# Memory's value projections moved from the front of the kernel to the dense blocks behind the mixer, with the front reordered and the convolution's taps dealt out anew

## The chip, the cores and the metric

The kernel runs on one core of a Trainium2 chip. The metric is the device time of one execution in microseconds, the median of several executions. The engines are TensorE (PE), VectorE (DVE), ScalarE (ACT), GpSimd (POOL) and SyncE (SP, which only issues transfers here). A 0.3% difference is about 3.9 us.

## What is computed

Two transformer blocks in a row on x (512 tokens by 1024), all in fp32. Of the reference only what the change touches is shown:

```python
# first block: adaptive norm, the front of the kernel
mod = c @ w_ada + b_ada                       # shift, scale, gate
h = rmsnorm(x, norm_g) * (1 + scale) + shift
proj = h @ w_in                               # q_a, k_a, v_a, z_a, ...

# second block: mixer's convolution branch and its end
c = u[..., :512] * sigmoid(u[..., 512:])
c = silu(layernorm(causal_dwconv(c, cv_dw_w) + cv_dw_b))   # 31 taps, 512 channels
y = concat([a, c]);  h = h + y @ w_out
# second block: cross attention to 256 memory rows
m = rmsnorm(mem, norm_mem_g)
kv = m @ w_ckv                                # 1024 columns of keys, 1024 of values
```

The memory's keys and values depend on the inputs `mem` and `w_ckv` alone, so they can be computed at any time before the cross attention.

## The kernel before, in words

**Products.** Each fp32 product is made of three matmuls on a high and a low part (high by high, high by low, low by high). Weights come in units of 512 KB: SP issues the load into `wr` (three buffers), ACT casts the high part `wh` (L162), DVE or POOL subtracts to get the low part `wl` (L163; a string of D and P says which engine takes which unit), then PE runs the unit's matmuls (L144). The load for a unit's buffer is issued when the unit three before it has been split.

**Front (L467 to L527).** An order written out by hand for all five engines. SP loads the vectors, the memory `mr`, x transposed (`xt`), 16 weight units for the memory and 16 rows `ar` for `mod`. A loop over n = 0 to 16 takes in each step one unit of memory weights: eight for keys (24 matmuls of 128x256 each), then eight for values (24 of 128x256 each, two units to a PSUM bank); results are copied out by ACT (`kvo`) and written to DRAM (`kv_d`) by DMAs that POOL issues. Between them stand, by tables of step numbers, the 16 rows of `mod` on DVE (`ada`, L440, one multiply and sum over 128x1024 each, ACT then forms shift or gain), the sums of squares of x (ACT squares, DVE adds to `xacc`) and of memory, the two inverse roots with their broadcasts (`bch`, `bcl`), and eight token chunks: `y` (DVE L462, one buffer in PSUM), high part (ACT L464), low part (DVE L466). The q and k projections of the first attention follow; the first of their transposes or the value projection (`z<-wh,h`) begins when they are done.

**Dense blocks (L1185 to L1221).** A list `BLOCKS` of weight units gives PE's order; `AFTER` names the attention steps that follow a unit. The convolution's 31 taps of each of four channel chunks are dealt to PE (units `cd`, 8 taps and 24 matmuls of 128x512 each), DVE (L1051, accumulating in PSUM) and POOL (L1046, with a product by ACT before it). A sum `ca` of both parts follows (L1057), then the layer norm over channels: the mean by PE (L1069), squares by ACT with 16 column sums on PE (`ones,cpr`), an inverse root, a broadcast and SiLU. Units `wo2a` multiply the attention half by `w_out`, units `wo2c` (L1232) the convolution half, and the cross attention's projections come next. DVE and POOL taps wait in two queues (`fill_v`, `fill_p`) from which some are issued after each unit.

## Time and profile before

| | |
|---|---|
| median of 3 runs | 1296.67 us (1294.57 to 1297.94) |
| the profiled execution | 1296.6 us, span 1294.8 us |
| mean granted TensorE clock | 0.971 of full speed |
| busy share of PE, DVE, ACT, POOL | 95%, 58%, 46%, 36% |
| DMA | 136.44 MB, mean 105 GB/s |

The profiled execution stands at the median, so a sum made against its trace can be read against the median as it is. PE is nearly always busy; it is below nine tenths in the first slices of the page (the front) and in those around 650 to 780 us (the end of the mixer), and the granted clock is below full in the same places. A matmul's busy time includes what overlaps with the next one; so the starts of matmuls, not their durations, tell how fast PE goes.

### The profile page before, as it was taken

What the parts mean: (1) busy time and instruction counts of PE and PEld (TensorE: products, weight loads), DVE (VectorE), ACT (ScalarE), POOL (GpSimd) and SP (SyncE); (2) the same over time, 40 slices, a digit from 0 to 9 for tenths busy, and PEclk for the clock granted to TensorE, in tenths of its full rate; (3) what the DMA queues carried; (4) which work ended last, traced back from release to release, by engine and by line L of the source; (5) the groups of instructions that cost most, each with busy time, mean ns of one, the idle gap of its engine ahead of it and who ended that gap; (6) DMA issues with size and microseconds to landing.
All of it is one profiled execution on the core that took longest, in us unless ns stands there. A gap on an engine that the chain in (4) does not pass through costs nothing.

```text
span 1294.8 us, 16902 instructions
## 1 busy us (share of the span) xinstructions
PE 1233.2 (95%) x6412; PEld 1039.3 (80%) x6412; DVE 750.5 (58%) x1216; ACT 601.6 (46%) x994; POOL 466.3 (36%) x315
## 2 busy tenths in 40 slices
PE   8799999999999999999899678999999999999996
PEld 6789887988887888899777566887888888888886
DVE  6654777666465174355877338456587777771112
ACT  7444557555652345264645436444444444442221
POOL 0573453332222138332537727104422222222222
PEclk8899999999999999999999779999999999999998
DMA  9853232232258432222122204312233333322221
GB/s 348 322 167 103 80 90 74 66 90 82 66 155 266 121 127 98 73 84 73 57 58 74 73 33 130 97 34 67 96 98 98 98 98 98 98 90 90 94 85 66
DMA packets 43859, 136.44 MB, mean 105 GB/s; under 512 B 4993, under 2 KB 8577, under 8 KB 43778
## 3 DMA queue, kind: packets, MB, share of 16 engines
q1 hardware_dynamic: 43010, 133.26, 32.3%
q0 software_dynamic: 768, 2.10, 0.4%
q8 instruction: 51, 0.84, 0.3%
q14 instruction: 30, 0.25, 0.1%
HBM read 125.90 MB, written 6.29 MB: 102 GB/s over the span
## 4 chain that ended last, share of the span: by engine, by line
PE 78%; DVE 9%; ACT 5%; POOL 4%; issue 3%; DMA 2%; SPq 0%; DVEq 0%; ACTq 0%; POOLq 0%
PE lin L144 64%; PE z L144 7%; PE pv L144 3%; PE sm L144 2%; DMA wr<-in_wts 1%; PE z L604 1%; POOL wl L163 1%; ACT wh L162 1%; DVE sm L1051 1%; DVE wl L163 1%; POOL rb L1046 1%; POOL nacc L1046 1%; DVE h L221 1%; DVE om L689 0%; DMA mr<-in_mem_t 0%
## 5 line engine op out<-in xcount | busy, mean ns | idle before, releaser
L144 PE MATMUL lin<-h,wh 128*128 128x512 f32 (+1 forms) x2264 | 699.0, 389 | 15.9 <-ACT wh L162 10.5
L144 PEld LDWEIGHTS lin<-h,wh 128*128 128x128 f32 x2264 | 420.4, 190 | 102.2 <-ACT wh L162 13.6
L163 POOL TENSOR_TENSOR wl<-wr,wh 128x1024 fp32r<-128x1024 f32 (+1 forms) x116 | 281.0, 2423 | 453.1 <-ACT wh L162 425.6
L144 PE MATMUL lin<-h,wl 128*128 128x512 f32 (+1 forms) x1132 | 437.6, 387 | 5.3 <-POOL wl L163 3.9
L162 ACT CAST wh<-wr 128x1024 fp32r<-128x1024 f32 (+1 forms) x198 | 205.5, 1041 | 266.2 <-PE lin L144 178.6
L144 PEld LDWEIGHTS lin<-h,wl 128*128 128x128 f32 x1132 | 215.1, 190 | 48.6 <-POOL wl L163 5.0
L163 DVE TENSOR_TENSOR wl<-wr,wh 128x1024 fp32r<-128x1024 f32 (+1 forms) x82 | 108.9, 1328 | 125.2 <-ACT wh L162 124.3
L144 PE MATMUL lin<-wh,h 128*128 128x256 f32 x672 | 130.3, 291 | 2.3 <-DVE h L985 2.3
L144 PEld LDWEIGHTS lin<-wh,h 128*128 128x128 f32 x672 | 109.5, 197 | 2.5 <-issue 2.4
L1346 DVE SCALAR_TENSOR_TENSOR cv<-up,vecs,cv 128x512 f32<-128x512 f32 x88 | 94.6, 1075 | 17.9 <-ACT cv L1344 16.4
L144 PE MATMUL lin<-wl,h 128*128 128x256 f32 x336 | 97.4, 290 | 1.8 <-POOL wl L163 1.8
L144 PE MATMUL lin<-zz,wh 128*128 128x512 f32 (+1 forms) x324 | 91.9, 369 | 0.0
L144 PEld LDWEIGHTS lin<-wl,h 128*128 128x128 f32 x336 | 66.3, 197 | 2.1 <-POOL wl L163 2.0
L144 PEld LDWEIGHTS lin<-zz,wh 128*128 128x128 f32 x324 | 58.1, 187 | 11.6
L144 PE MATMUL lin<-zz,wl 128*128 128x512 f32 (+1 forms) x162 | 59.7, 369 | 0.0
L317 POOL TENSOR_TENSOR nacc<-nacc,sq 128x512 f32<-128x512 f32 x34 | 53.4, 1578 | 15.9 <-ACT sq L316 15.4
L1341 POOL MEMSET up<- 128x2 f32 x44 | 4.3, 100 | 148.7 <-DVE cv L1346 116.6
L675 POOL TENSOR_TENSOR zs<-zs,y 64x512 f32<-64x512 f32 x16 | 26.4, 1653 | 72.4 <-DVE y L674 70.0
L1353 ACT ACTIVATE cv<-cv 128x512 f32<-128x512 f32 x22 | 13.9, 632 | 60.0 <-DVE cv L1346 60.0
L689 DVE TENSOR_TENSOR_SCAN om<-om 128x511 f32<-128x511 f32 (+3 forms) x32 | 36.7, 1187 | 8.4 <-ACT om L685 8.1
L1342 DVE TENSOR_TENSOR up<-lin,rb 128x512 f32<-128x512 f32 x44 | 30.1, 686 | 16.3 <-PE lin L144 13.7
L214 DVE TENSOR_TENSOR tl<-z,th 128x512 fp32r<-128x512 f32 (+1 forms) x60 | 33.3, 595 | 10.8 <-ACT th L213 10.4
(392 smaller groups left out, 1701.2 us busy)
## 6 DMA issues: line engine op xcount, KB each, us to landing
wr<-in_wts SPq DMA_DIRECT2D x198, 512.0 KB, 3.5
ar<-in_wts SPq DMA_DIRECT2D x16, 512.0 KB, 6.3
qk<-qk SPq DMA_DIRECT2D x24, 128.0 KB, 2.3
wr<-in_wts SPq DMA_DIRECT2D x8, 384.0 KB, 3.0
xt<-in_x_t SPq DMA_DIRECT2D x4, 512.0 KB, 8.2
kv_d<-kvo POOLq DMA_DIRECT2D x16, 128.0 KB, 4.9
ma_d<-gt SPq DMA_DIRECT2D x8, 256.0 KB, 4.4
ma<-ma_d SPq DMA_DIRECT2D x8, 256.0 KB, 2.9
```

Of the source, the lines that this page charges most:

```text
L144: pe.matmul(o, lhsT=lhsT, rhs=rhs, start=start, stop=stop, skip_group_check=True)
L162: act.copy(out=hi[:, :n], in_=raw[:, :n])
L163: lo_engine().tensor_tensor(out=lo[:, :n], in0=raw[:, :n], in1=f32(hi[:, :n]), op=ALU.subtract)
L214: dve.tensor_tensor(out=lo, in0=src, in1=f32(hi), op=ALU.subtract)
L221: dve.scalar_tensor_tensor(out=lo, in0=src, scalar=g, in1=f32(hi), op0=ALU.mult, op1=ALU.subtract)
L317: pool.tensor_tensor(out=acc, in0=acc, in1=q, op=ALU.add)
L675: pool.tensor_tensor(out=zs[r], in0=zs[r], in1=y[r], op=ALU.mult)
L689: dve.tensor_tensor_scan(out=om[:, o:e], data0=om[:, o:e], data1=om[:, o:e], initial=1.0, op0=ALU.mult, op1=ALU.bypass)
L1046: pool.tensor_tensor(out=cb_, in0=cb_, in1=pr, op=ALU.add)
L1342: dve.tensor_tensor(out=up[:, :T], in0=o, in1=rb[:, 0], op=ALU.mult)
L1346: dve.scalar_tensor_tensor(out=r, in0=up[:, 2 - j:2 - j + T], scalar=V("ffn_w", c * 3 + j), in1=r, op0=ALU.mult, op1=ALU.add)
L1353: act.activation(out=a, in_=a, func=AF.Silu)
```

## The change

- The front computes only the eight key units (`N_FRONT` 8). Its low parts are made by DVE for the first two units and by POOL for six.
- x's sums of squares are formed by PE: ACT squares eight chunks into buffers, PE sums each over the channels by a column of ones. Memory's squares are summed the same way, 16 such matmuls in place of three DVE adds and two matmuls; DVE copies the result to `mrc`. The inverse root and the broadcast of `mrc` are written later in the program, but are not under the manual order, and stand in the front of DVE all the same.
- The rows of `mod` are loaded earlier and come two to a step; the token chunks start at step 4 instead of 9.
- The memory's split tiles (hi and lo, 2.1 MB) are written to DRAM (`ms_d`) by eight DMAs of SP and read back in the dense blocks by eight more (`memory_back`).
- Eight units `mv` (24 matmuls of 128x256 each) stand between the last blocks of `BLOCKS`.
- Unit `cd:4` is gone: each chunk has eight taps on PE. Of chunks 2 and 3 DVE gets 14 taps each (before 12 and 4), POOL 9 each (before 11).
- The low parts of the last blocks alternate between POOL and DVE (`B2_LO`); the steps of the layer norm come after `wo2a:0`, `wo2a:1` and `mv:6`, and only the first of them flushes the queues.

```diff
-CV_UNITS = (1, 1, 1, 2)
+CV_UNITS = (1, 1, 1, 1)
-START_LO = "DDDDDDDDPPPPPPPP"
+START_LO = "DDPPPPPP"
+N_FRONT = 8
-ADA_LOADS = (2, 1, 1, 2, 1, 1, 2, 1, 1, 2, 1, 1)
-NORM_AT = (6, 9)
-H_AT = (9, 10, 11, 12, 13, 14, 16, 16)
+SQ_AT = (0, 0, 1, 1, 1, 2, 2, 2)
+ADA_LOADS = (4, 2, 2, 2, 2, 2, 2)
+NORM_AT = (3, 5)
+H_AT = (4, 5, 5, 6, 6, 7, 8, 8)
-B2_LO = "P"
+B2_LO = 26 * "P" + 5 * "PD"
-CONV_POOL = (8, 8, 11, 11)
+CONV_POOL = (8, 8, 9, 9)
-          "u2:7 cd:2 cd:3 cd:4 wo2a:0 wo2a:1 wo2a:2 wo2a:3")
+          "u2:7 cd:2 mv:0 cd:3 mv:1 mv:2 mv:3 wo2a:0 mv:4 wo2a:1 mv:5 wo2a:2 mv:6 wo2a:3 mv:7")
-         21: "n3", 22: "o3", 27: "l0", 28: "l1"}
+         21: "n3", 22: "o3", 28: "l0", 30: "l1", 33: "l2"}
...
     def memory_norm():
         o = ps_sm()
-        for i in range(2):
-            mm(o[:, i:i + 1], raws[0][:, i * P:(i + 1) * P], ones[:, 0:1], True, True)
-        rsq(mrc, o[:, :2], D)
+        for k in range(KD):
+            for i in range(2):
+                mm(o[:, i:i + 1], raws[k // 4][:, (k % 4) * NM + i * P:(k % 4) * NM + (i + 1) * P], ones[:, 0:1],
+                   k == 0 and i == 0, k == 7)
+        dve.tensor_copy(out=mrc, in_=o[:, :2])
...
+    def sums_x(k, q):
+        for i in range(NT):
+            mm(xs_[:, i:i + 1], q[:, i * P:(i + 1) * P], ones[:, 0:1], k == 0 and i == 0, k == 7)
...
+    for i, t in enumerate(mt):
+        nc.sync.dma_start(out=ms_d[i], in_=f32(t))
...
+    def memory_back():
+        for i in range(4):
+            hi, lo = htile(), htile()
+            nc.sync.dma_start(out=f32(hi), in_=ms_d[2 * i])
+            nc.sync.dma_start(out=f32(lo), in_=ms_d[2 * i + 1])
...
-            fill(FILL_P if i < 22 else 5, fill_p)
-        norm_out()
+            fill(FILL_P if i < 22 else 4, fill_p)
```

In the changed kernel the line numbers differ: L440 becomes L412, L462 and L466 become L435 and L439, L1046 becomes L1060, L163 becomes L166.

SP's queue in the front, before, from the memory's load on (`mr` memory, `wr` weight units, `xt` chunks of x, `lamt` and `posi` small inputs, `ar` rows of `mod`):

```order
L349 DMA mr<-in_mem_t 128x4x256 x2
L149 DMA wr<-in_wts 128x1024 x2
L448 DMA xt_83<-in_x_t 128x2x512
L149 DMA wr<-in_wts 128x1024
L448 DMA xt_83<-in_x_t 128x2x512 x2
L712 DMA lamt<-in_lam 128x256
L725 DMA posi<-in_pos 128x4
L149 DMA wr<-in_wts 128x1024
L448 DMA xt_83<-in_x_t 128x2x512
L149 DMA wr<-in_wts 128x1024 x2
L435 DMA ar<-in_wts 128x1024 x2
L149 DMA wr<-in_wts 128x1024
```

The same stretch of SP's queue in the changed kernel:

```order
L353 DMA mr<-in_mem_t 128x4x256 x2
L152 DMA wr<-in_wts 128x1024 x2
L420 DMA xt_83<-in_x_t 128x2x512
L152 DMA wr<-in_wts 128x1024
L420 DMA xt_83<-in_x_t 128x2x512 x2
L505 DMA ms_d<-h 128x512 x8
L693 DMA lamt<-in_lam 128x256
L706 DMA posi<-in_pos 128x4
L152 DMA wr<-in_wts 128x1024
L420 DMA xt_83<-in_x_t 128x2x512
L152 DMA wr<-in_wts 128x1024 x2
L407 DMA ar<-in_wts 128x1024 x4
```

The eight writes of `ms_d` stand ahead of the fourth weight unit, and four rows `ar` come at once where two came before.

DVE's queue in the front, before, from the second pair of `mod` rows (`ar,mod`) behind x's inverse root to the row behind the first `y`; `rv`, `rq` and `mrc` are the memory's inverse root:

```order
L440 SCALAR_TENSOR_TENSOR ar,mod<-ar,cb 128x1024 x2
L294 TENSOR_TENSOR bcl<-xrc,bch 128x4
L440 SCALAR_TENSOR_TENSOR ar,mod<-ar,cb 128x1024 x2
L287 TENSOR_SCALAR rv<-sm 128x2
L262 RECIPROCAL mrc<-rq 128x2
L263 TENSOR_TENSOR rq<-mrc 128x2
L264 TENSOR_TENSOR rq<-rq,rv 128x2
L265 TENSOR_SCALAR rq<-rq 128x2
L266 TENSOR_TENSOR mrc<-mrc,rq 128x2
L440 SCALAR_TENSOR_TENSOR ar,mod<-ar,cb 128x1024
L462 SCALAR_TENSOR_TENSOR y<-xt_83,gain,xrb 128x512
L440 SCALAR_TENSOR_TENSOR ar,mod<-ar,cb 128x1024
```

DVE in the changed kernel, the same stretch, with the copy of the memory's sums (`mrc<-sm`):

```order
L412 SCALAR_TENSOR_TENSOR ar,mod<-ar,cb 128x1024 x2
L297 TENSOR_TENSOR bcl<-xrc,bch 128x4
L412 SCALAR_TENSOR_TENSOR ar,mod<-ar,cb 128x1024 x2
L435 SCALAR_TENSOR_TENSOR y<-xt_83,gain,xrb 128x512
L375 COPY mrc<-sm 128x2
L412 SCALAR_TENSOR_TENSOR ar,mod<-ar,cb 128x1024
L439 SCALAR_TENSOR_TENSOR h<-y,shift,h 128x512
L412 SCALAR_TENSOR_TENSOR ar,mod<-ar,cb 128x1024
L290 TENSOR_SCALAR rv<-mrc 128x2
L435 SCALAR_TENSOR_TENSOR y<-xt_83,gain,xrb 128x512
L265 RECIPROCAL mrc<-rq 128x2
L266 TENSOR_TENSOR rq<-mrc 128x2
```

Eight rows of `mod` and one `y` now stand ahead of DVE's first step on the memory's sums, where six rows stood before; behind it are eight rows, seven `y` and eight low parts, where ten, eight and eight were.

POOL at the end of the mixer, before, from the first tap of chunk 2 (`rb`; chunk 3 is `nacc`) to the first low parts of the attention half of `w_out`:

```order
L1046 TENSOR_TENSOR rb<-rb,cpr 128x512 x4
L163 TENSOR_TENSOR wl<-wr,wh 128x1024
L1046 TENSOR_TENSOR rb<-rb,cpr 128x512 x5
L163 TENSOR_TENSOR wl<-wr,wh 128x1024
L1046 TENSOR_TENSOR rb<-rb,cpr 128x512
L1046 TENSOR_TENSOR nacc<-nacc,cpr 128x512 x10
L163 TENSOR_TENSOR wl<-wr,wh 128x1024 x3
```

POOL in the changed kernel, the same stretch (`kv_d` are the values' way to DRAM):

```order
L1060 TENSOR_TENSOR rb<-rb,cpr 128x512 x3
L166 TENSOR_TENSOR wl<-wr,wh 128x1024
L1060 TENSOR_TENSOR rb<-rb,cpr 128x512 x4
L166 TENSOR_TENSOR wl<-wr,wh 128x1024
L1060 TENSOR_TENSOR rb<-rb,cpr 128x512
L1060 TENSOR_TENSOR nacc<-nacc,cpr 128x512 x3
L964 DMA kv_d<-kvo 128x256 x2
L1060 TENSOR_TENSOR nacc<-nacc,cpr 128x512 x4
L166 TENSOR_TENSOR wl<-wr,wh 128x1024
L1060 TENSOR_TENSOR nacc<-nacc,cpr 128x512
L964 DMA kv_d<-kvo 128x256 x2
L166 TENSOR_TENSOR wl<-wr,wh 128x1024 x2
```

Of 20 sums of taps 16 are left; one more low part stands between them, and four issues of transfers among and behind them.

## Rows read from the trace of the kernel before

**Rows 1.** The page: granted TensorE clock in tenths, 40 slices of the span.

```profile
PEclk8899999999999999999999779999999999999998
```

**Rows 2.** Busy time by stretch: us, engines' busy us (instructions), clock, DMA share, GB/s.

```profile
60.00:90.00 30.00, 25.77 (x149) 22.87 (x149) 20.43 (x32) 13.98 (x25) 21.33 (x17) 0.90 0.58 192
...
726.00:742.00 16.00, 7.00 (x16) 5.07 (x17) 6.38 (x7) 6.24 (x8) 12.10 (x8) 0.57 0.17 51
742.00:754.00 12.00, 11.04 (x42) 7.44 (x40) 2.30 (x4) 2.09 (x2) 4.74 (x2) 1.00 0.28 108
754.00:770.00 16.00, 9.79 (x43) 9.33 (x44) 7.47 (x22) 5.39 (x8) 2.34 (x1) 0.55 0.10 33
```

**Rows 3.** Groups by line, DVE, 0 to 90 us: busy us, mean ns | idle before.

```profile
L440 DVE SCALAR_TENSOR_TENSOR ar<-ar,cb 128x1024 f32<-128x1024 f32 x16 | 19.0, 1214 | 0.0
L163 DVE TENSOR_TENSOR wl<-wr,wh 128x1024 fp32r<-128x1024 f32 x8 | 9.7, 1224 | 2.5 <-ACT wh L162 2.1 <-ACT kvo L399 0.3
...
L466 DVE SCALAR_TENSOR_TENSOR h<-y,shift,h 128x512 fp32r<-128x512 f32 x8 | 6.0, 747 | 3.6 <-ACT h L464 3.6
```

**Rows 4.** Timeline, end of the front, DVE then PE: start, us, instruction [idle before].

```profile
78.29 0.75 DVE L462 SCALAR_TENSOR_TENSOR y<-xt,gain,xrb 128x512 f32<-128x512 f32 x1
...
83.52 0.75 DVE L466 SCALAR_TENSOR_TENSOR h<-y,shift,h 128x512 fp32r<-128x512 f32 x1 [2.18 <-ACT h L464]
...
88.90 0.39 PE L144 MATMUL lin<-h,wh 128*128 128x512 f32 x1
89.13 0.39 PE L144 MATMUL lin<-h,wl 128*128 128x512 f32 x1
89.36 0.40 PE L144 MATMUL z<-wh,h 128*128 128x256 f32 x2
```

**Rows 5.** DMA, 0 to 90 us: GB/s in 40 slices, packets and bytes.

```profile
GB/s 25 237 320 347 383 400 377 391 411 411 415 357 361 413 415 402 379 308 118 266 350 260 404 375 340 373 148 359 388 328 119 138 211 138 2 215 169 204 113 127
DMA packets 9114, 25.87 MB, mean 287 GB/s; under 512 B 1169, under 2 KB 2705, under 8 KB 9106
```

**Rows 6.** Timeline, PE: first and last matmuls of a memory unit, memory's sums.

```profile
47.42 0.33 PE L144 MATMUL lin<-wh,h 128*128 128x256 f32 x1
...
50.22 0.28 PE L144 MATMUL lin<-wh,h 128*128 128x256 f32 x1
50.34 0.50 PE L144 MATMUL sm<-ones,mr 128*128 128x1 f32 x4
```

**Rows 7.** PE's waits, 690 to 800 us: total, times, longest.

```profile
PE lin L144 <- ACT wh L162: 7.8, 1, 7.8
...
PE lin L144 <- POOL wl L163: 2.1, 1, 2.1
...
PE z L144 <- DVE wl L163: 1.7, 1, 1.7
```

**Rows 8.** Timeline, POOL: first tap of chunk 2, chunk 3's taps, two low parts.

```profile
702.31 2.65 POOL L1046 TENSOR_TENSOR rb<-rb,cpr 128x512 f32<-128x512 f32 x2 [2.73 <-ACT cpr L1045]
...
720.36 13.48 POOL L1046 TENSOR_TENSOR nacc<-nacc,cpr 128x512 f32<-128x512 f32 x10
733.81 4.69 POOL L163 TENSOR_TENSOR wl<-wr,wh 128x1024 fp32r<-128x1024 f32 x2
```

**Rows 9.** Timeline, PE, end of the mixer.

```profile
736.21 0.80 PE L144 MATMUL lin<-h,wl 128*128 128x512 f32 x1 [2.11 <-POOL wl L163]
...
755.09 6.63 PE L144 MATMUL z<-ones,cpr 128*128 128x1 f32 x32 [2.04 <-ACT cpr L1077]
...
768.80 1.22 PE L144 MATMUL lin<-h,wh 128*128 128x512 f32 x2 [2.27 <-ACT h L213]
...
794.86 0.61 PE L144 MATMUL z<-h,wh 128*128 128x512 f32 x2
```

**Rows 10.** Groups by line, PE, 696 to 800 us: the mean's matmuls.

```profile
L1069 PE MATMUL z<-ca,ones 128*128 128x512 f32 x8 | 3.6, 592 | 0.0
```

**Rows 11.** The page, DMA issues: transfers, KB each, median us from issue to landing.

```profile
kv_d<-kvo POOLq DMA_DIRECT2D x16, 128.0 KB, 4.9
```

More of the change, by code (lines that the diff above doesn't have):

```diff
@@ L320, in block_kernel @@
     kv_d = dramp.tile([4, P, D], F32, name="kv_d")
+    ms_d = dramp.tile([8, P, T], F32, name="ms_d")
     ma_d = dramp.tile([KD, P, T], F32, name="ma_d")
@@ L495, in block_kernel @@
         mem_split(1)
-        rest = []
-        for n in range(17):
-            if n < 16:
-                mem_split(n + 2)
+        rest, xq = [], {}
+        xs_ = ps_sm()
+        for n in range(9):
+            mem_split(n + 2)
             if n < len(ADA_LOADS):
@@ L502, in block_kernel @@
                     ada_load()
-            if n == 0:
-                memory_squares()
-            if 1 <= n <= 4:
-                squares_x(2 * n - 2)
-                squares_x(2 * n - 1)
-            out_ = mem_unit(n) if n < 16 else lambda: None
+            for k in range(KD):
+                if SQ_AT[k] == n:
+                    xq[k] = squares_x(k)
+            if n == NORM_AT[1] - 1:
+                for raw in raws:
+                    act.activation(out=raw, in_=raw, func=AF.Square)
+            out_ = mem_unit(n) if n < N_FRONT else lambda: None
+            for k in range(KD):
+                if SUM_AT[k] == n:
+                    sums_x(k, xq.pop(k))
             if n == NORM_AT[0]:
-                rsq(xrc, col_sums([xacc]), D)
-            if n == NORM_AT[0] + 2:
+                rsq(xrc, xs_[:, :NT], D)
+            if n == NORM_AT[0] + 1:
                 bcast_mm(xrc, xrb)
@@ L519, in block_kernel @@
                     ada(i)
+                    if rest:
+                        rest.pop()()
             out_()
-            while rest:
-                rest.pop()()
             for j in range(KD):
@@ L708, in block_kernel @@
             nxt = qk("qa", "ka", p + 1)
+    rsq(mrc, mrc, D)
+    bcast(mrc, mrb, 2)
     lamt = smp.tile([P, T], F32, tag="sq", name="lamt")
@@ L948, in block_split, with memory_values @@
         if i < len(blocks):
+            lo_seq[:] = B2_LO[i], -1
             split_of[i] = split(raw_of.pop(i))
             block_load(i + 3)
+    ms2, mbank = [], [None]
+    def memory_back():
[3 more added lines that the diff above has]
+            nc.sync.dma_start(out=f32(lo), in_=ms_d[2 * i + 1])
+            ms2.extend((hi[:, e * NM:(e + 1) * NM], lo[:, e * NM:(e + 1) * NM]) for e in range(2))
+    def memory_values(n, w):
+        wh, wl = w
+        if n == 0:
+            memory_back()
+        h, kk = n // 2, n % 2
+        if kk == 0:
+            mbank[0] = ps_lin()
+        o = mbank[0]
+        for j in range(4):
+            k = 4 * kk + j
+            xh, xl = ms2[k]
+            c = slice(j * 256, (j + 1) * 256)
+            for i in range(2):
+                oo = o[:, i * 256:(i + 1) * 256]
+                t = slice(i * P, (i + 1) * P)
+                mm(oo, xh[:, t], wh[:, c], k == 0 and i == 0, False)
+                mm(oo, xh[:, t], wl[:, c], False, False)
+                mm(oo, xl[:, t], wh[:, c], False, k == 7)
+        if kk:
+            q = smp.tile([P, T], F32, tag="sq", name="kvo")
+            act.copy(out=q, in_=o)
+            for i in range(2):
+                nc.gpsimd.dma_start(out=kv_d[2 + i, :, h * 256:(h + 1) * 256], in_=q[:, i * 256:(i + 1) * 256])
     def projected(name, half, kk, w):
@@ L1211, in block_kernel @@
             for st_ in AFTER.get(i, "").split():
+                if st_ == "l0":
+                    fill(99)
                 if st_[0] == "l":
[L1213 removed]
                     norm[int(st_[1])]()
```

67 lines of the change are left out of this document (16 added, 51 removed).

## The prediction, made before the changed kernel was run

> **What bounds the kernel now.** I read the page first, then the busy time by stretch, then the waits and timelines of the two stretches that the change touches. In the page's clock line [rows 1] the reader is to see that PE runs at the full level nearly everywhere, and that the two dips are at the start and just behind the middle: a gain must come from there, or PE's work must shrink. By the change PE's work shrinks by one unit of taps only (24 matmuls of 128x512, one every 0.23 us [rows 4]: 5.6 us); the value units are moved, not removed. So the sum is about where PE's idle time lies.
>
> In the front, from 60 to 90 us, PE is busy 25.8 of 30 us but the clock is 0.90, DVE 20.4 and the DMA engines 0.58 [rows 2]: no one engine is full, and a chain decides. The end of that chain is on DVE: the last `y` starts at 78.29, the last low part at 83.52, and the first matmul behind the q and k projections at 89.36 [rows 4]. Before 40 us the transfers are full: some 400 GB/s in most slices up to 38 us [rows 5]. At the mixer's end PE is idle twice: from 725 to 736, where it waits 7.8 us for a cast and 2.1 for a low part [rows 7] that POOL could only make behind 20 taps (the last ten take 13.5 us, up to 733.8 [rows 8]); and around the layer norm's sums, where it stands at the 1.2 GHz level (clock 0.57 in 726 to 742, 0.55 in 754 to 770) and is busy 7.0 and 9.8 of 16 us [rows 2].
>
> **The front, part by part.** *DVE.* Removed: six low parts at 1.23 us (7.4), seven adds of x's squares (by the 128x512 row, 0.75 each: 5.2), three adds of memory's squares (1.23 for the largest by the 128x1024 row, half and a quarter with overhead for the others: 2.4) [rows 3]. That is 15 us, all of it ahead of the memory's inverse root; if DVE never waited in their place the front would end 15 us earlier. It will wait. The copy `mrc<-sm` is in DVE's queue behind eight rows of `mod` and one `y`, and it needs 16 column sums on PE, which stand behind key unit 5, which stands behind x's broadcast. Before, that point came early: the sums started at 50.34 [rows 6] and were two. Now I estimate: the broadcast of x ends at about 48.6, where it now ends at 47.4 with the unit behind it [rows 6] (ACT's queue holds two memory squares, a cast and a key copy between the inverse root and `bch`); unit 5 takes 2.9 us at full clock (47.42 to 50.34 [rows 6]) and up to 5.0 below it, so it ends at 52 to 53.6; 16 sums take 6.63 us at the end of the mixer, at the lower level [rows 9], and by half 3.3. The copy then runs at 56 to 59; I take 57. Behind it DVE has eight rows of `mod` at 1.2 us (9.5), seven `y` and eight low parts at 0.7, the row's 0.75 less what overlaps (10.5) [rows 3], 2.5 of small operations and 1.5 of waits on ACT's high part (estimates; such waits are 3.6 in all now [rows 3]): 24. The last low part ends at about 81, where it now ends at 84.3. PE is less behind then: before, the q and k projections had 5.1 us of matmuls left after it (to 89.36 [rows 4]), because value units were in their way; now they lack only the last chunk, six matmuls, 1.4 us. So the first `z` starts at about 82.3: **a gain of 7 us**. Ends: 3 (copy at 59, all the front at the lower level) and 28 (the transfers alone, next).
>
> *Transfers.* The front moves 25.87 MB in 90 us [rows 5]. Four MB of value weights go, 2.1 MB of writes come, and they stand ahead of the fourth weight unit, so that unit and all rows of `mod` are 2.1 MB / 0.4 = 5.3 us further down the queue than they would be. By bytes alone the last row of `mod` has 20.3 MB ahead: 2.1 MB go in the first four slices (9 us), the rest at 400 GB/s ends at 54.5, and the first `z` would follow at about 61.5, 28 us earlier than now: the far end. The rows of this trace show 400 to 415 GB/s in the slices of 20 to 38 us [rows 5]. The Trainium skill, DMA: Bandwidth & Descriptors, Specifications, gives a core about 358 GB/s from HBM, which the trace does not bear out; by it that far end would be 60, and the 28 would be 22.
>
> **The mixer's end, part by part.** *POOL.* 16 sums of taps instead of 20 at 1.35 [rows 8]: 21.6; three low parts between them, one more than before, 2.4 each: 7.2; one pair of transfers to issue, 1.1. From 702.3, where its first tap starts now, that is 732.2, against 733.8 [rows 8]. The extra 12 DVE taps at 0.75 lie beside it. So the convolution's sums are ready 1 us earlier, and `wo2a:0`'s low part, ahead of the last tap, at 730.9. *PE before that* has `mv:0`, `cd:3`, `mv:1` to `mv:3` (5.6 and four times 2.9) in a stretch of 28 us: they fit in the holes and cost nothing, whatever the reads of `ms_d` do within a few us. If they came 10 us late, that would no longer be so. *PE behind it* is now the bound, and I add it up. `wo2a:0` restarts after a hole, at the lower level for some 4 us, as the unit at 736.21 does [rows 2, 9]: 5.6 + 2 = 7.6, to 738.5. The mean, 3.6 us of overlapping matmuls [rows 10] and 3.0 from start to start: 741.5. `mv:4` 2.9, `wo2a:1` 5.6: 750. A wait of 2 for the first square, as now, and 6.6 for the sums [rows 9]: 758.7. `mv:5` at the lower level 5.0, `wo2a:2` 5.6, `mv:6` 2.9: 772.2. Broadcast 0.9, `wo2a:3` 5.6, `mv:7` 2.9: 781.6. Now `wo2c` runs: 96 matmuls, 22.2, and 2.3 of wait at its start as now [rows 9]: 806.1, where the next product begins at 794.9 [rows 9]. Behind it a wait of 1.7 for a low part [rows 7] is covered: **9.5 us later**. If every step ran at full clock, 2.0 less for `wo2a:0`, 3.3 for the sums and 2.1 for `mv:5`: 2.1. I take **8**, near the upper end, since the lower level around the sums has its own row [rows 2], and only `mv:5`'s share is inferred from it.
>
> **Sum.** Minus 7 and plus 8 from the profiled 1296.6, which is the median's 1296.67: **1297.5 us**. Nothing between the two places changes its order; the layers behind the second are the same.
>
> **The rivals.** *The front packs.* ACT and PE keep ahead, DVE meets its copy without waiting, and the 15 us come out whole: 1296.6 - 15 + 8 = 1290. For it: DVE is the engine at the end of the chain and loses 15 us of work. Against it: in-order DVE behind 16 sums. *The end stays at full clock.* The value units fill the holes, so that PE never falls to 1.2 GHz there: -7 + 2 gives 1292. For it: from 742 to 754, when PE is busy 11.0 of 12 us, the clock is 1.00 [rows 2]. Against it: column sums keep PE mostly idle, and the clock fell while they ran. The Trainium skill, TensorE: Matmul & The Clock Gate, What's actually happening, has the level follow how busy the engine has been; by that rule filled holes would bring this rival's time, and the trace agrees with the rule in both stretches just named. *Slower:* the chain on PE at the end costs its full 10, and a wait is added behind it: the cross attention's key and value split waits for `mv:7`'s way through DRAM (4.9 us to land [rows 11], and a read), which holds the buffer that the next weights need. It decides if those weights land after `wo2c` ends, about 806; I put them at 805 to 808, so up to 2 us. With a front that gains 4: 1296.6 - 4 + 12 = 1304.5. *It does not do what it says:* the writes of `ms_d` take back the bandwidth that the value weights left, the rows of `mod` come no earlier, and the inverse root of `mrc` still stands in DVE's front queue. Gain 3, cost 8: 1301.5.
>
> **How the numbers follow.** A measurement tells 0.3%, 3.9 us, from no change. My forecast's own sum has 0.44, of which 0.30 fall within 3.9 us and 0.07 on either side; the packed front 0.22, faster; the end at full clock 0.14, half of it faster by more than 3.9 us; the long end 0.14 and the writes 0.06, slower. Faster 0.36, same 0.37, slower 0.27. The range takes in the packed front with some of the transfers' end (1286) and the long end (1304).
>
> **What would show it.** Right: the copy of the memory's sums waits 5 us or more on DVE; the first `z` at 81 to 84; POOL's last tap at 732 less the front's gain; the mean 6 us earlier against the taps; `wo2c` beginning after `mv:7` with no wait of more than 1.5, and ending 24 to 26 us behind it; a clock near 0.6 while the column sums run. Wrong: the first `z` before 78 (the front packs) or after 87 (the writes); a clock of 1.00 from the mean to `wo2c`; a wait of several us at `mv:0` on the read tiles that delays `wo2a:0`; PE idle for more than 2 us between `wo2a:0` and `wo2c`.

## The result and the profile after: 0.8% slower

| | before | after |
|---|---|---|
| median | 1295.64 us (5 runs, 1294.57 to 1297.94) | 1306.70 us (5 runs, 1304.12 to 1308.59) |
| ratio to before, 95% interval | | 1.0078 [1.0059, 1.0097] |
| profiled execution, its span | 1296.6, 1294.8 | 1306.7, 1304.9 |
| mean granted clock | 0.971 | 0.968 |
| busy PE, DVE, ACT, POOL | 95%, 58%, 46%, 36% | 96%, 58%, 46%, 35% |

The forecast was 1297.5, so no change, with a range up to 1304. The kernel became 11.1 us slower by the medians, and the profiled execution 10.1 us longer, which is the sum that the places below have to make up. PE's busy line and the clock line of the page of the changed kernel answer to [rows 1]:

```profile
PE 1249.7 (96%) x6472; PEld 1054.7 (81%) x6472; DVE 758.0 (58%) x1218; ACT 598.2 (46%) x989; POOL 459.0 (35%) x311
...
PEclk8689999999999999999898899999999999999998
```

PE is busier by 16.5 us than before (1233.2), though the change removes PE's unit of taps; its idle time, the span less this, fell by 6.4 only (61.6 to 55.2). So PE spends more time at its work: 12.5 us of it are the column sums of the front (13.9 us by their groups, 1.4 before), the rest matmuls at a lower clock. The clock has a new dip in the second slice, which is the front.

**The front** gained 5.2 us in this execution, where 7 was forecast. Timeline of the changed kernel, DVE and PE (start, us, instruction, idle before it and its releaser), in place of [rows 4]:

```profile
57.53 0.16 DVE L375 COPY mrc<-sm 128x2 f32<-128x2 f32 x1 [7.67 <-PE sm L147]
...
81.39 0.75 DVE L439 SCALAR_TENSOR_TENSOR h<-y,shift,h 128x512 fp32r<-128x512 f32 x1 [0.81 <-ACT h L437]
...
84.15 0.28 PE L147 MATMUL z<-wh,h 128*128 128x256 f32 x1
```

The copy of the memory's sums waits 7.67 us, and it comes at 57.5 where 57 was forecast; the last low part ends at 82.1 where 81 was forecast. The first `z` comes at 84.15 and not 82.3. One execution is little to go by here: experiments 1, 3, 4 and 11 have the same front, and their first `z` comes at 83.15, 82.38, 83.12 and 82.03, so the forecast lies within what executions differ by. The busy time by stretch has the columns of [rows 2], for the front and for the end of the mixer:

```profile
40.00:60.00 20.00, 17.08 (x95) 16.68 (x95) 8.61 (x18) 7.77 (x14) 8.19 (x5) 0.67 0.89 348
60.00:90.00 30.00, 26.84 (x139) 22.57 (x138) 23.05 (x41) 14.79 (x28) 15.44 (x12) 0.83 0.34 101
...
742.00:754.00 12.00, 9.96 (x48) 9.34 (x47) 4.40 (x13) 2.52 (x4) 0.00 (x0) 0.67 0.13 45
754.00:770.00 16.00, 16.00 (x91) 14.39 (x91) 7.22 (x13) 7.49 (x9) 3.50 (x3) 0.93 0.44 127
770.00:796.00 26.00, 20.86 (x97) 16.68 (x96) 19.92 (x17) 13.15 (x18) 16.95 (x10) 0.96 0.29 104
```

PE stands at a clock of 0.67 in 40 to 60 us and 0.83 in 60 to 90, where it had 0.90 in the latter [rows 2]; from the end of the last low part to `z` it takes 2.0 us, where I gave it 1.3. At the end of the mixer, PE is busy all of 754 to 770, as the change means it to be; but behind that, in 770 to 796, where from 774.6 on nothing but the convolution half `wo2c` should run, it is idle for 5 of 26 us.

**The end of the mixer** lost nearly twice the forecast. Timeline of PE in the changed kernel, in place of [rows 9]:

```profile
697.75 0.58 PE L147 MATMUL lin<-wh,h 128*128 128x256 f32 x1 [4.82 <-DMA h<-ms_d]
...
724.48 0.80 PE L147 MATMUL lin<-h,wl 128*128 128x512 f32 x1 [2.61 <-POOL wl L166]
...
745.71 6.68 PE L147 MATMUL z<-ones,cpr 128*128 128x1 f32 x32 [2.04 <-ACT cpr L1091]
...
774.57 0.63 PE L147 MATMUL lin<-h,wh 128*128 128x512 f32 x2
...
778.33 0.98 PE L147 MATMUL lin<-h,wh 128*128 128x512 f32 x2 [1.36 <-ACT h L216]
...
794.24 1.22 PE L147 MATMUL lin<-h,wh 128*128 128x512 f32 x2 [3.78 <-DVE xr L1248]
...
804.28 0.51 PE L147 MATMUL z<-h,wh 128*128 128x512 f32 x1 [0.16 <-ACT wh L165]
...
806.05 0.50 PE L147 MATMUL z<-h,wl 128*128 128x512 f32 x1 [1.03 <-DVE wl L166]
```

The last broadcast ahead of the mixer's end, first before, then after, is 6.0 us earlier:

```profile
697.92 0.22 PE L144 MATMUL lin<-identr,bch 128*128 128x128 f32 x1
```

```profile
691.92 0.22 PE L147 MATMUL lin<-identr,bch 128*128 128x128 f32 x1
```

`wo2c` begins at 774.57, 5.8 us later than before; the walk along PE gave 781.6, less these 6 us 775.6. Up to there the walk holds within 1 us. Then `wo2c` lasts until 804.28: 29.7 us, where 24.5 were forecast. The next product begins 9.4 us later than before, so the stretch from the broadcast to it, the mixer's end, takes 112.4 us in place of 96.9 and costs 15.4. This is no chance of one execution: the stretch takes 112.7 to 112.8 in experiments 2, 3 and 6, and 96.9 in experiment 10, whose edits leave PE's order in it as it is.

What held `wo2c` is on DVE. PE waits for `xr` (the residual sum that frees a bank of PSUM), which stands in DVE's queue behind a low part. The timelines of DVE and POOL of the changed kernel over the same stretch:

```profile
783.97 9.61 DVE L224 SCALAR_TENSOR_TENSOR h<-xr,vecs,h 128x512 fp32r<-128x512 f32 x1 [0.79 <-ACT h L223]
...
784.73 2.41 POOL L1268 TENSOR_TENSOR kvl<-wr,kvh 128x1024 fp32r<-128x1024 f32 x1
787.11 2.38 POOL L166 TENSOR_TENSOR wl<-wr,wh 128x1024 fp32r<-128x1024 f32 x1
789.46 1.28 POOL L320 TENSOR_TENSOR nacc<-nacc,sq 128x512 f32<-128x512 f32 x1
790.70 2.33 POOL L1268 TENSOR_TENSOR kvl<-wr,kvh 128x1024 fp32r<-128x1024 f32 x1
795.60 1.28 POOL L320 TENSOR_TENSOR nacc<-nacc,sq 128x512 f32<-128x512 f32 x1 [2.57 <-ACT sq L319]
```

An operation of 128x512 that lasts 0.75 us elsewhere (L439 above) lasts 9.61 here, and ends 0.6 us after a run of POOL operations without a gap: a product (L1266, 782.36 to 784.7) was under way as it began, and the first four rows of POOL above followed. The same operation lasts 9.59 to 9.63 us in experiments 2, 3, 4 and 6. In the kernel before, POOL ran without a gap in this place too, from 779.23 to 790.2, and began with the low parts `kvl` of the cross attention's keys; the longest DVE operation beside it lasted 2.85 us:

```profile
779.23 4.79 POOL L1252 TENSOR_TENSOR kvl<-wr,kvh 128x1024 fp32r<-128x1024 f32 x2 [16.25 <-ACT kvh L1251]
```

```profile
781.71 2.85 DVE L221 SCALAR_TENSOR_TENSOR h<-xr,vecs,h 128x512 fp32r<-128x512 f32 x1 [1.06 <-ACT h L220]
```

So a run of POOL without a gap is not enough to make nine microseconds of it. What is new in this place is the first step of the keys' split, a product on POOL. Two rows of it, first of the kernel before, then of the changed one:

```profile
750.83 2.40 POOL L1250 TENSOR_TENSOR wr<-wr,mrb 128x1024 f32<-128x1024 f32 x1 [3.37 <-DMA wr<-kv_d]
```

```profile
778.87 2.41 POOL L1266 TENSOR_TENSOR wr<-wr,mrb 128x1024 f32<-128x1024 f32 x1 [3.24 <-issue]
```

The products ran in POOL's idle time at 751 and 761 before, under the layer norm. Now they run at 779 and 782, under `wo2c`: by the program their buffers `wr` are those of the value units' weights, which hold them until `mv:7`. The Trainium skill, SBUF — State Buffer, Who interferes with whom, says that VectorE and GpSimd share a port pair under an exclusive lock, so that the second waits until the first has finished. That an operation of DVE waits, the row of 9.61 us shows; that it waited through four of POOL's, the page does not say.

One more piece lies further on. The feed-forward part before and after, the same ten microseconds of work, first before, then after:

```profile
891.00:901.00 10.00, 10.00 (x46) 8.27 (x45) 6.54 (x5) 2.48 (x4) 5.06 (x3) 1.00 0.46 159
```

```profile
900.00:910.00 10.00, 10.00 (x38) 8.07 (x38) 5.53 (x3) 1.11 (x2) 4.91 (x3) 0.84 0.44 157
```

PE was busy without a break in both, and the granted clock was 0.84 in the second: 10 us at 0.16 less is 1.6 us. PE's pauses just ahead are the same in both kernels, 1.35 us in all. Experiments 2, 3 and 11 show 0.83 in 900 to 910, experiments 1 and 8 show 1.00; what lowers it stays open. From the next product to the end the changed kernel takes 500.6 us, the kernel before 499.9.

The sum against the forecast: ahead of the mixer's end 1.0 less gain (6.0 against 7), the mixer's end 7.4 more (15.4 against 8), and 0.7 behind it, which makes 9.1, the difference between the forecast +1 and the measured +10.1.

### The profile page after: what moved, and what is told of

It is laid out like the page before. It is cut to its first block, busy times and chain, and to the rows that moved or that the text cites. A ratio compares the mean times of both kernels' runs of the same rounds, so it can differ in the third digit from the quotient of the medians.

```text
span 1304.9 us, 17038 instructions
## 1 busy us (share of the span) xinstructions
PE 1249.7 (96%) x6472; PEld 1054.7 (81%) x6472; DVE 758.0 (58%) x1218; ACT 598.2 (46%) x989; POOL 459.0 (35%) x311
## 4 chain that ended last, share of the span: by engine, by line
PE 79%; DVE 9%; ACT 4%; issue 3%; DMA 2%; POOL 2%; SPq 0%; DVEq 0%; POOLq 0%; ACTq 0%
PE lin L147 65%; PE z L147 7%; PE pv L147 3%; PE sm L147 3%; PE z L581 1%; DVE sm L1065 1%; DMA wr<-in_wts 1%; DVE ar L412 1%; DMA ms_d<-h 1%; POOL rb L1060 1%; POOL nacc L1060 1%; POOL wl L166 1%; ACT wh L165 0%; DVE h L224 0%; DMA mr<-in_mem_t 0%
## 5 line engine op out<-in xcount | busy, mean ns | idle before, releaser
L147 PE MATMUL lin<-h,wh 128*128 128x512 f32 (+1 forms) x2264 | 708.0, 393 | 11.5 <-DVE xr L1248 3.8
L147 PEld LDWEIGHTS lin<-h,wh 128*128 128x128 f32 x2264 | 426.5, 194 | 98.6 <-ACT wh L165 5.6
L166 POOL TENSOR_TENSOR wl<-wr,wh 128x1024 fp32r<-128x1024 f32 (+1 forms) x116 | 280.5, 2418 | 491.1 <-ACT wh L165 475.3
L147 PEld LDWEIGHTS lin<-h,wl 128*128 128x128 f32 x1132 | 218.8, 193 | 49.1 <-POOL wl L166 5.2
L166 DVE TENSOR_TENSOR wl<-wr,wh 128x1024 fp32r<-128x1024 f32 (+1 forms) x81 | 109.0, 1347 | 123.1 <-ACT wh L165 122.7
L147 PE MATMUL lin<-zz,wl 128*128 128x512 f32 (+1 forms) x162 | 59.7, 369 | 0.0
L320 POOL TENSOR_TENSOR nacc<-nacc,sq 128x512 f32<-128x512 f32 x34 | 51.8, 1533 | 21.4 <-ACT sq L319 21.1
L1369 ACT ACTIVATE cv<-cv 128x512 f32<-128x512 f32 x22 | 13.9, 632 | 59.8 <-DVE cv L1362 59.8
```

The costliest lines, as they stand in the source:

```text
L147: pe.matmul(o, lhsT=lhsT, rhs=rhs, start=start, stop=stop, skip_group_check=True)
L166: lo_engine().tensor_tensor(out=lo[:, :n], in0=raw[:, :n], in1=f32(hi[:, :n]), op=ALU.subtract)
L320: pool.tensor_tensor(out=acc, in0=acc, in1=q, op=ALU.add)
L1369: act.activation(out=a, in_=a, func=AF.Silu)
```

## The experiments

Ratios are to the kernel before, run on the same chip beside it, with medians of 1295.6 to 1297.4; "after" is the changed kernel, 1306.7, which was not run beside them, so that a difference of 2 us from it tells nothing. Places inside a kernel are read from its one profiled execution. The stretch from the first `z` to the last broadcast ahead of the mixer's end, whose work is nearly the same in all, lasts 605.5 to 612.4 us in them, so I compare stretches and not times since the start.

**1. The keys' low part on DVE.** If the collision costs what the wait shows, taking POOL's part of it away gives it back.

```diff
-            pool.tensor_tensor(out=lo, in0=raw, in1=f32(hi), op=ALU.subtract)   # L1268
+            dve.tensor_tensor(out=lo, in0=raw, in1=f32(hi), op=ALU.subtract)
```

> The changed kernel, with the low parts of the memory's keys (two subtractions of 128x1024 behind wo2c) made by DVE in place of POOL. In the changed kernel POOL runs four sums without a gap from 784.7 to 793.0, two of them these, and one DVE low part of 128x512 that takes 0.75 us elsewhere lasts 9.61; PE then waits 3.78 for xr. Theory (DVE's instruction with two operands in SBUF is held off as long as POOL's run of sums lasts): without two of the four the run is broken, the DVE instruction takes under 4 us, the wait for xr falls under 1 and the time by 3 to 4 us to about 1303. Rival (the wait is only the queue: DVE is behind because wo2c's inputs came late): the long instruction stays over 7 us, and 2.5 us of added DVE work make it 1307 to 1309.

Measured: 1301.31 us (10 runs), ratio 1.0035 [1.0018, 1.0051], 5.4 us less than after. The long wait is gone, three short ones for `xr` stand there (1.27, 0.83 and 0.23). But the next product now waits, as PE's timeline shows, and DVE was itself held:

```profile
778.75 5.80 DVE L1268 TENSOR_TENSOR kvl<-wr,kvh 128x1024 fp32r<-128x1024 f32 x1
```

```profile
801.17 0.51 PE L147 MATMUL z<-h,wl 128*128 128x512 f32 x1 [2.29 <-DVE wl L166]
```

From the start of `wo2c` (770.81) to this point (801.17) are 30.4 us, against 31.5 in after (774.57 to 806.05): the place itself gave back 1.1. The profiled execution is 7.7 us shorter than that of after; 3.8 of it lie ahead of `wo2c`, in steps that the edit doesn't touch, and 2.8 behind this place, where the low clock at 900 us (1.6) is missing. So 3.9 us are left from `wo2c` on, about what the theory named; why most of them lie behind the place stays open.

**2. The memory's sums later.** The copy on DVE would not wait if it stood behind more rows and chunks.

```diff
-NORM_AT = (3, 5)
+NORM_AT = (3, 8)
```

> The changed kernel, with the memory's sums of squares and DVE's copy of them moved from step 5 to step 8 of the front. In the changed kernel DVE waits 7.7 us for that copy at 49.9 to 57.5, with eight rows of mod queued behind it. Theory (the copy's place in DVE's queue holds the front): the wait is gone, the rows run from 50 on, and the first z starts 4 to 6 us earlier, near 79; the whole kernel gains as much, 1301 to 1303. Rival (the rows of mod or PE's low clock hold the front): the first z moves by less than 1.5 us and the time stays within 2 us of 1306.7.

Measured: 1309.48, ratio 1.0102 [1.008, 1.0124]. The median is 2.8 us above after. The first `z` came at 85.12, not earlier; the copy still waits 6.1 us, now at 73.3, because PE's sums had also moved, behind the first units of the q projection. The wait was only moved.

**3. The read of the tiles one unit earlier.** PE waits 4.82 us for the tiles `ms_d`.

```diff
+            if i == 22:
+                memory_back()
...
-        if n == 0:
-            memory_back()
```

> The changed kernel, with the eight reads of ms_d issued one unit earlier (ahead of the weight load that waits for a split). In the changed kernel PE waits 4.8 us for them at 692.9. Theory (the end of POOL's taps sets wo2a:0, and the reads cost nothing): the wait shrinks to under 2 us, but wo2a:0 still waits for its low part until 724 less at most 1, and the time stays within 1.5 us of 1306.7. Rival (the reads are on the path): 3 to 5 us less, 1302 to 1304.

Measured: 1305.44, ratio 1.0071 [1.0048, 1.0094]; the interval overlaps that of after. The wait for `ms_d` is gone from the list of PE's waits between 690 and 800, and `wo2a:0` starts at 725.18 behind POOL's low part (2.59 us), as it did at 724.48. So this wait lay in a hole that POOL's taps leave, as forecast.

**4. The old deal of taps** in the changed kernel (the fifth unit on PE and 11 taps of chunks 2 and 3 on POOL, as before).

```diff
-CV_UNITS = (1, 1, 1, 1)
+CV_UNITS = (1, 1, 1, 2)
-CONV_POOL = (8, 8, 9, 9)
+CONV_POOL = (8, 8, 11, 11)
-          "u2:7 cd:2 mv:0 cd:3 mv:1 ...
+          "u2:7 cd:2 mv:0 cd:3 cd:4 mv:1 ...
```

(The steps of the layer norm and the string of low parts shift by the one unit.)

> The changed kernel with the convolution's taps dealt as before: unit cd:4 back on PE (5.6 us at full clock), POOL 11 taps and DVE 12 and 4 for chunks 2 and 3. Theory (POOL's taps set wo2a:0, PE has room before it): POOL has four sums more, 5.4 us, so wo2a:0 and all behind it come 4 to 6 us later, 1311 to 1313. Rival (PE's work sets the end, and POOL is hidden): 5.6 us of PE work more and no other effect, also later, but with no wait for POOL's low part before wo2a:0; a third reading, that the added DVE taps cost more than they bring, gives 1303 or less.

Measured: 1317.68, ratio 1.0172 [1.0149, 1.0195], 11 us more than after. PE's waits from 690 to 800 us (total, times, longest) in this kernel:

```profile
PE lin L147 <- ACT wh L165: 9.1, 1, 9.1
PE lin L147 <- DMA h<-ms_d: 5.1, 1, 5.1
PE lin L147 <- DVE wl L166: 5.0, 1, 5.0
```

The direction was the theory's, but its size (4 to 6) was half of what came. The sign of the rival stands too: no wait for POOL's low part ahead of `wo2a:0`. PE's 9.1 us for a cast are the 7.8 of [rows 7] again. In the kernel before, ACT's rows at that cast are:

```profile
731.18 0.72 ACT L1045 ACTIVATE cpr<-cp,vecs 128x512 f32<-128x512 f32 x1 [0.63 <-POOL nacc L1046]
731.80 2.92 ACT L162 CAST wh<-wr 128x1024 fp32r<-128x1024 f32 x3
```

ACT makes the products for POOL's taps one at a time, each after a wait for POOL, and the cast of PE's next weights stands behind the last of them.

**5. No values at all.** The value units are taken out of the list, so this kernel leaves out the projection of the memory's values, with its reads, splits and copies; the front is kept, writes included.

```diff
-          "u2:7 cd:2 mv:0 cd:3 mv:1 mv:2 mv:3 wo2a:0 mv:4 wo2a:1 mv:5 wo2a:2 mv:6 wo2a:3 mv:7")
+          "u2:7 cd:2 cd:3 wo2a:0 wo2a:1 wo2a:2 wo2a:3")
```

(All low parts of the last blocks are POOL's; the steps of the layer norm come after `wo2a:0`, `wo2a:1` and `wo2a:3`.)

> The changed kernel without the eight units mv and the reads of ms_d: it leaves out the projection of the memory's values (tiles of the split memory are written in their place, so that the transfers of the front are the same). It prices the value units at the mixer's end. Theory (the end is PE's own sum once POOL's taps are done): the four units behind wo2a:0, 13.6 us, go from PE; part of that comes back as the wait for the layer norm and its channels; wo2c then ends some 11 to 14 us earlier, and the time is 1292 to 1296. Rival (the value units lie in holes): 1302 to 1306.

Measured: 1286.27, ratio 0.9923 [0.9905, 0.9942], 20.4 us less than after. PE's timeline of this kernel:

```profile
722.11 2.07 PE L1083 MATMUL z<-ca,ones 128*128 128x512 f32 x2 [9.68 <-DVE ca L1071]
...
756.60 0.96 PE L147 MATMUL lin<-h,wh 128*128 128x512 f32 x3 [2.89 <-ACT h L216]
...
783.88 0.61 PE L147 MATMUL z<-h,wh 128*128 128x512 f32 x2
```

The last part of the mean ends at 724.2 (after: 735.3), `wo2c` begins at 756.6 (after: 774.6), and the next product at 783.9 (after: 804.3). Eight units of 2.9 us are 23.2 us of PE's work, and 20.4 us came out. So hardly any of it was hidden, not even the four units that stand in holes ahead of the mean. Without them `wo2a:0` runs there, from 700.55 to 706, ahead of the end of the taps (720.2); in after it starts at 724.48, behind them. PE still waits 12.1 us for the convolution. The value units took a place that `wo2a:0` fills by itself. The theory's 11 to 14 had counted those four at nothing.

**6. The memory's sums early.**

```diff
-NORM_AT = (3, 5)
+NORM_AT = (3, 3)
```

> The changed kernel with the memory's sums of squares at step 3 of the front in place of 5, so that the eight rows of mod no longer stand behind a copy that waits for key unit 5. With the sums at step 8 the wait only moved, because the sums then stood behind q's first units in PE's queue. Theory (DVE's queue holds the front): the wait of 7.7 falls under 2, the first z starts 4 to 7 us earlier than 84.2, the time is 1300 to 1303. Rival (PE below full clock and the weights hold the front): z not before 82.5, the time 1305 to 1307.

Measured: 1305.43 (6 runs, 1300.94 to 1310.65), ratio 1.0069 [1.0042, 1.0096]; from after it cannot be told. The copy waits 3.0 us instead of 7.7, but the first `z`, at 82.50, stays within the 82.0 to 84.2 of the kernels with after's front: the sums now take 6.95 us (from 38.55) ahead of a memory unit and of x's broadcast, which ends at 53.1 instead of 48.7. The rival that PE itself is late fits both numbers.

**7. DVE beside a run of POOL, by itself.** Four sums of 128x1024 on POOL back to back, three operations of 128x512 on DVE beside them, at the very start.

```diff
+        for _ in range(4):
+            pool.tensor_tensor(out=ta[2], in0=ta[0], in1=ta[1], op=ALU.add)
+        dve.tensor_tensor(out=td, in0=ta[0][:, :T], in1=ta[1][:, :T], op=ALU.add)
+        dve.tensor_tensor(out=td, in0=ta[0][:, :T], in1=ta[1][:, :T], op=ALU.add)
+        dve.tensor_scalar(out=td, in0=ta[0][:, :T], scalar1=2.0, scalar2=1.0, op0=ALU.mult, op1=ALU.add)
```

> The changed kernel with a small experiment at its start, before the memory lands: POOL runs four sums of 128x1024 with two operands in SBUF without a gap; meanwhile DVE has two sums of 128x512 with two operands in SBUF and then one operation with one such operand. Theory (held off as long as POOL's run lasts): DVE's first sum lasts until the fourth POOL sum ends, 7 to 9.5 us, the second 0.7. Rival 1 (held off to the end of the POOL sum under way): the first lasts up to 3 us, the second again up to 3. Rival 2 (no contention): 0.7 each. The whole time is later by what POOL and DVE spend here and says nothing.

Measured, the timeline of both engines:

```profile
4.58 10.48 POOL L456 TENSOR_TENSOR ta<-ta,ta 128x1024 f32<-128x1024 f32 x4 [4.13 <-DVE ta L453]
...
6.92 0.68 DVE L457 TENSOR_TENSOR td<-ta,ta 128x512 f32<-128x512 f32 x1
7.63 2.72 DVE L458 TENSOR_TENSOR td<-ta,ta 128x512 f32<-128x512 f32 x1
10.39 2.47 DVE L459 TENSOR_SCALAR td<-ta 128x512 f32<-128x512 f32 x1
12.78 2.31 DVE L463 SCALAR_TENSOR_TENSOR gain<-vecs 128x8 f32<-128x8 f32 x1
```

POOL's four run on at 2.6 us each. DVE's operations end at 7.6, 10.4, 12.9 and 15.1, which is about one for each of POOL's: a DVE operation gets in near the end of the POOL operation under way, and the next one is held until the following end. Not the whole run was waited for, so the first rival holds and the theory falls in this form. Why one operation lasted through four in the changed kernel is left open.

**8. Three repairs together:** experiment 1 (its line is not shown again), experiment 6, and the low part of `wo2a:0` on DVE, with that of `mv:4` on POOL in exchange.

```diff
-NORM_AT = (3, 5)
+NORM_AT = (3, 3)
-B2_LO = 26 * "P" + 5 * "PD"
+B2_LO = 26 * "P" + "PDDPPDPDPD"
```

> Three edits on the changed kernel at once: the keys' low parts on DVE, the memory's sums at step 3, and the low part of wo2a:0 on DVE in place of POOL (mv:4's on POOL), so that it doesn't wait behind the taps. Theory: 4 to 6 for the first, 4 to 6 for the second, 2 to 3 for the third, 1292 to 1297, level with the kernel before or a little faster. Rival (the pieces hide one another): 1299 to 1303.

Measured: 1300.96 (10 runs), ratio 1.0027 [1.0009, 1.0046]. The first `z` is at 81.20 and `wo2c` at 766.67, both as wanted, but the median is that of experiment 1 alone, as the rival that the pieces hide one another has it. How they would is not shown: the profiled execution, 1296.39, is the fastest of the ten, and in it the mixer's end is 6.9 us shorter than in after.

**9. The taps alone,** in the kernel before: nothing else of the change.

```diff
-CV_UNITS = (1, 1, 1, 2)
+CV_UNITS = (1, 1, 1, 1)
-CONV_POOL = (8, 8, 11, 11)
+CONV_POOL = (8, 8, 9, 9)
-          "u2:7 cd:2 cd:3 cd:4 wo2a:0 wo2a:1 wo2a:2 wo2a:3")
+          "u2:7 cd:2 cd:3 wo2a:0 wo2a:1 wo2a:2 wo2a:3")
-         21: "n3", 22: "o3", 27: "l0", 28: "l1"}
+         21: "n3", 22: "o3", 26: "l0", 27: "l1"}
```

> The kernel before with the taps of the change alone: no unit cd:4, DVE 14 and POOL 9 taps for chunks 2 and 3; the values stay in the front. Theory (POOL's taps set the end of the mixer, the moved values brought the loss): POOL ends its taps 5.4 us earlier, and the mean, the sums and wo2c follow: 4 to 6 us faster than before, 1290 to 1292. Rival (the taps gain nothing without the value units that fill PE): within 1.5 us of before, 1295 to 1298.

Measured: **1286.01** (5 runs, 1285.53 to 1290.79), ratio 0.993 [0.9908, 0.9952]: faster than both kernels. Two rows of PE's timeline:

```profile
738.87 2.07 PE L1069 MATMUL z<-ca,ones 128*128 128x512 f32 x2 [7.11 <-DVE ca L1057]
...
763.41 1.22 PE L144 MATMUL lin<-h,wh 128*128 128x512 f32 x2 [2.28 <-ACT h L213]
```

The cast and the low part that PE waited 9.9 us for [rows 7] are not waited for any more; three `wo2a` units run from 712.7 to 729.0 without a hole, and then PE waits 7.1 for the convolution. `wo2c` begins 5.4 us earlier than before [rows 9]. The profiled execution, 1290.79, was the slowest of the five, and its clock line has dips of a tenth in slices 13 and 21 that [rows 1] lack: up to the last broadcast, at 702.01, it is 4.1 us later than before. From there to the next product it takes 87.5 us in place of 96.9, and these 9.4 us are the median's 9.8, twice the size that the theory named.

**10. The sums by PE alone,** in the kernel before: x's and memory's squares summed by PE, DVE's adds removed.

```diff
-        dve.tensor_tensor(out=xacc, in0=xacc, in1=q, op=ALU.add)
+    def sums_x(k, q):
+        for i in range(NT):
+            mm(xs_[:, i:i + 1], q[:, i * P:(i + 1) * P], ones[:, 0:1], k == 0 and i == 0, k == 7)
```

(and the 16 sums of memory as in the change.)

> The kernel before with the sums of squares by PE alone: eight chunks of x and of the memory summed by columns of ones on PE, seven and three DVE adds of the front gone; tables, values and taps as before. Theory (DVE is the front's chain and loses 7.2 us of work): the first z 3 to 6 us earlier than 89.4, 1290 to 1293. Rival (PE's sums, at 0.2 to 0.4 us each, 48 of them, push PE's front back by as much): the first z within 1.5 us, 1295 to 1298.

Measured: 1301.91 (10 runs), ratio 1.0031 [1.0012, 1.005], 6 us slower by the medians. The first `z` is at 94.32, 5 us later than before. DVE lost 7.9 us of work up to 90 us (51.8 busy against 59.7) and turned it into waiting; its waits there (2.1 each in the kernel before):

```profile
DVE wl L163 <- ACT wh L162: 13.2, 5, 4.4
DVE rv L287 <- PE sm L144: 5.9, 1, 5.9
```

PE is busy 20.8 us of 38 to 60, against 16.2 before. The theory, that relieving DVE shortens the front, failed, and the time lies above the rival's range too: the sums stand in PE's order, and everything behind them waits.

**11. The keys' split behind the next product's order,** in the changed kernel.

```diff
-    kvs = []
-    for i in range(4):
...
     nxt = cross_q(0)
+    kvs = []
+    for i in range(4):
...
```

> The changed kernel with the splits of the memory's keys and values written behind the first cross-attention query instead of ahead of it, so that POOL's run of two products, two low parts and a sum no longer falls into wo2c. In the changed kernel PE waited 3.78 us there for xr behind a DVE low part that lasted 9.61, and wo2c took 29.7 us for 22.2 of matmuls. Theory (those two engines' collision is that wait): the low part lasts under 3 us, wo2c 24 to 26, the time 1301 to 1304. Rival (wo2c waits for its own channels, not for POOL): wo2c over 28, the time within 1.5 of 1306.7; a third outcome, that the keys now come too late for the first scores, would show as a PE wait for kvl.

Measured: 1304.9 (5 runs), ratio 1.0064 [1.0042, 1.0085]. The collision is gone: `wo2c` runs from 775.37 to 799.24, 23.9 us, as the theory has it (its time, up to 1304, is just missed), and the longest low part lasts

```profile
791.52 2.88 DVE L224 SCALAR_TENSOR_TENSOR h<-xr,vecs,h 128x512 fp32r<-128x512 f32 x1
```

But the median is less than 2 us below after, within the intervals: by 826 us PE stands where it stood in after, having waited for a low part of `h` (2.8 in two waits) and for a cast (1.9). The mixer's end is 5.8 us shorter than in after, and from there to the end of the kernel it takes 5.5 more. I read this as the same work of POOL, ACT and DVE that had to be done ahead of the scores in either order; what is shown is that the time came back as other waits.

**12. The layer norm two units earlier,** in experiment 9's kernel.

```diff
-         21: "n3", 22: "o3", 26: "l0", 27: "l1"}
+         21: "n3", 22: "o3", 24: "l0", 25: "l1"}
...
-                    fill(99)
+                    if st_ == "l0":
+                        fill(99)
```

> As the run with the taps alone, and the layer norm's mean and squares after wo2a:0 and wo2a:1 in place of wo2a:2 and wo2a:3, as the changed kernel has them, still with the values in the front. Theory: the wait for the norm is covered by the two units behind it, another 3 to 6 us: 1285 to 1290, faster than both kernels. Rival (the mean then stands on PE before POOL's taps are done, and PE waits as long there): as the taps alone or up to 3 us slower.

Measured: 1290.83 (10 runs), ratio 0.9961 [0.9942, 0.998], 5 us slower than experiment 9, where the rival allowed 3. The mean, set earlier in PE's order, waits 12.1 us for the convolution (7.1 in experiment 9) with the units that could run meanwhile queued behind it; the mixer's end takes 89.9 us against 87.5. The rival was right in kind.

## Why the prediction was wrong

Four medians part the taps from the rest of the change. The taps are worth −9.8 us in the kernel before (experiment 9) and −11.0 in the changed one (experiment 4); the rest costs +20.7 with the new deal of taps (after against experiment 9) and +20.3 with the old one (experiment 4 against the kernel before). Experiment 5 splits the rest: +0.3 from experiment 9 to the kernel without any values, and +20.4 for the values at the end.

The +0.3 hides two larger sums. By stretches of the profiled executions, in us:

| | to the first `z` | to the last broadcast | the mixer's end | to the end |
|---|---|---|---|---|
| before | 89.4 | 608.6 | 96.9 | 499.9 |
| taps alone (9) | 89.6 | 612.4 | 87.5 | 499.5 |
| no values (5) | 83.0 | 607.0 | 94.0 | 499.5 |
| after | 84.2 | 607.8 | 112.4 | 500.6 |

From experiment 9 to 5 the front gains 6.6, and the mixer's end loses 6.5 without any value unit in it. Experiment 12 shows 2.5 of this as the price of the earlier layer norm; the rest is not taken apart. The rows of experiments 9 and 5, apart from those shown above:

```profile
89.59 0.40 PE L144 MATMUL z<-wh,h 128*128 128x256 f32 x2
...
702.01 0.22 PE L144 MATMUL lin<-identr,bch 128*128 128x128 f32 x1
...
789.50 0.61 PE L144 MATMUL z<-h,wh 128*128 128x512 f32 x2
```

```profile
82.96 0.28 PE L147 MATMUL z<-wh,h 128*128 128x256 f32 x1
...
689.91 0.22 PE L147 MATMUL lin<-identr,bch 128*128 128x128 f32 x1
```

Against the forecast, the mixer's end cost 7.4 more: 5.2 in `wo2c`, 3.2 in the discount taken from the walk, less the 1.0 by which the walk up to `wo2c` was too long. Term by term:

- *The taps.* Forecast: POOL's last tap 1 us earlier, and no time named for it alone. That POOL's end moves little is right (725.7 measured, 725 forecast with the front's gain). But the worth of the new deal lay in PE's 9.9 us of waits for ACT and POOL, which vanish, and in 5.6 us of PE's work, less the 7.1 us that PE then waits for the convolution. I set this gain against the value units in one walk and never priced it by itself, so it stood in no sum as what the change gives away.
- *"They fit in the holes and cost nothing".* This was the step that hid the loss. As times the walk was right: PE waits 4.82 us for the reads and `wo2a:0` starts at 724.48. As a price it was wrong: experiment 5 shows the mean ending 11.2 us earlier without the values, of which 2.0 were there at the last broadcast. The holes were PE's wait for casts and low parts behind the taps; with the new deal of taps `wo2a` units fill them (experiments 5 and 9).
- *From the mean to `wo2c`.* Within 1 us. The sums took 6.68 us against 6.6, at a clock of 0.67 over 742 to 754, and the rival with the full clock at the end is refuted there.
- *"Now `wo2c` runs: 96 matmuls, 22.2, and 2.3 of wait".* **This term failed**: 29.7 instead of 24.5. The 2.3 us of wait were 1.4; the rest is the 3.78 us for `xr` and the restart behind it, at a clock of 0.85 from 794.2 to 804.3, some 1.5 us. My slow rival named the right place, the cross attention's split, and its time, 1304.5, lies near the measured one by luck: its mechanism was late loads for up to 2 us and a front that gains 4, where the operations themselves were in one another's way. Experiment 11 limits the worth of this: with the long wait gone, the 5.8 us came back as waits behind it, so what the stretch up to 826 us is bound by stays open.
- *The discount from 11.2 to 8.* 1.7 for a covered wait and 1.5 for a higher clock. The wait for the low part only fell from 1.7 to 1.03, and the clock stayed low in 742 to 754. The raw walk, 11.2, would have been the better term.
- *The front, 7.* It gained 5.2 to 7.3 in the five kernels that have it, so the term was right as far as such executions tell. The copy (57) and its wait (5 or more) were right; in after the last low part ended 1.1 us later than forecast, and `z` came 2.0 behind it, not 1.3, with PE at 0.50 to 0.56, near the 1.2 GHz level, from 78 us on, of which I had allowed for the memory unit alone. The transfers' own end, 61.5, lies far off; of [rows 5]'s slices from 20 to 38 us, two stand at 357 and 361 GB/s, not at the 400 to 415 that I read. The rivals that the front packs (`z` before 78) and that nothing changes in it (after 87) are both out. Experiment 10 shows that the sums by PE, which I counted as 7.6 us off DVE, cost 5 to 6 us in the old order.
- *What was not foreseen at all:* 1.6 us of lower clock at 900 to 910 us. It is 0.7 behind the next product in all, and the times of one kernel spread by 2 to 5 us on either side of its median.

What stays open: why a DVE operation lasted through four POOL operations in five kernels, when the same pattern by itself lets about one in at each, and POOL's run in the kernel before held none for more than 2.85 us; why experiment 1 gains more behind the place that it changes than in it; and what bounds PE between `wo2c` and 826 us once that wait is gone. Moving the values with the old front's sums was not tried.
